# Combined weights of the first two up-projection column tiles, kept in memory apart from the normed x

## The chip, the cores and the metric

The kernel runs on one core of one Trainium2 chip. Its time is the device time of one execution in microseconds (us). A core has five engines that work side by side, each through its own list of instructions: the tensor engine (PE, matmuls and transposes, results in PSUM), the vector engine (DVE), the scalar engine (ACT), GpSimd (POOL) and the sync engine (SP), which here only issues DMA transfers. They wait for one another by semaphores.

## What is computed

Two layers of a transformer trunk on x of 1024 positions by 1024 channels. In each layer a modulated norm and a mixer (attention in layer 0, retention and a state-space model in layer 1) are followed by another modulated norm and a convolutional feed-forward part. The change touches the first half of the last one, the "up" product, and the modulation vector:

```python
def modulated_rmsnorm(x, g, shift, scale):
    y = rmsnorm(x, g) * (1.0 + scale.astype(jnp.float32)[:, None, :]) + shift.astype(jnp.float32)[:, None, :]
    return y.astype(x.dtype)

def conv_ffn(h, w_in, conv_w, conv_b, w_out):
    up = h @ w_in
    val, gate = jnp.split(up, 2, axis=-1)
    gate = lax.conv_general_dilated(gate, conv_w[:, None, :], (1,), [(CONV_W - 1, 0)],
                                    dimension_numbers=('NWC', 'WIO', 'NWC'),
                                    feature_group_count=D_FF) + conv_b
    return (jax.nn.gelu(gate) * val) @ w_out

# in reference(), for each layer i
    mod = cond @ mod_w[i] + mod_b[i]
    sh1, sc1, g1, sh2, sc2, g2 = jnp.split(mod, 6, axis=-1)
```

D_FF is 2816, so `up` has 22 column tiles of 128 for `val` and 22 for `gate`.

## The kernel before

**Precision.** Every matmul operand is split into a high part (`fp32r`, by an ACT copy, L124) and a low part (the rest, a DVE subtraction, L125), and a product is three passes: high by high, high by low, low by high (`mm3`, L134 to L136). A product of four tiles of 128 channels is 12 matmuls of 128x512.

**Order.** The program is written in one sequence; a scheduler puts each engine's instructions into a fixed order when the kernel is built, by the priorities (`high_priority` lifts an operation by `AHEAD` places) and by which buffers are free. Tiles come from pools; a tile with a tag waits until an earlier tile of the same tag (`bufs` of them) has been read for the last time. The chip then runs each engine's list in that order.

**The up phase** (`up7`, L1494) runs once in each layer, here called the first (from about 642 us) and the second (from about 1809 us). It forms the product of two 2x2 block matrices with seven products instead of eight. For column tile `ft` the weights are `g` (of gate) and `a` (of val), each 1024 columns in memory, the first 512 of them for the channels 0 to 511 ("lo"). The blocks of x are B11, B12, B21, B22 and the combinations T1 to T4 of them, kept as high and low parts: B11 and B21 in `h[0]`, T1 and T3 in `h[1]` (both called `h` in rows), B22 in `X0`, T4 and T2 in `X2` (both called `X` in rows). Per column tile:

- `head`: loads g and splits it as A; `p1` = A lo by B11, copied to `s1` by ACT (L1534); `p2` = A hi by B21 (`c1`).
- `sums` (L1540): loads a; four DVE operations of 512 columns (L1545 to L1549) make s3 = g lo − a lo, a combined V and a combined G; V and G are split by L124 and L125.
- `p5` = V lo by T1, `p3` = G hi by B22, `p6` = G lo by T2, `p7` = S3 by T3 (S3 is the split of s3, made in `third`, L1587), `p4` = V hi by T4. `gate0` (L1572) adds p1 and p2 and starts the convolution; `last` finishes the second half.

For the first four tiles (`PRE`) `head`, `p1` and `p2` run first, among the making of the blocks (`up7_blocks`, L1457, a generator whose pieces `next(prep)` lets in). The making normalizes half of xT in place (`scale`), subtracts blocks from each other (L1482, L1486, L1487, L1489, 2048 columns each) and splits each result (`low`, L1479 on ACT and L1480 on DVE): T1, B22, T2, T3, T4. Then `free()` gives xT's memory back, and the pool `late` takes it: V (L1547), `s3h` and `s3l`, the convolution's `ca` and others lie there. PSUM has two banks `c1`, three `c2`, three `c3`; `p1` and `p2` take `c1`, `p6`, `p7`, `p4` and the block making take `c2`, `p5` and `p3` take `c3`. The tag `ma` (2 buffers) holds in turn the sum of squares, s3 and gate0's sum.

**The modulation sums.** `mod_slow` (L535) makes columns of the modulation vector in small steps: one load of 256 KB of `mod_w` into `ms` and one DVE operation into `md` per step (L551, L553), and four matmuls at the end of a column (`mod_cols`). A step is let in by `mod_on`: one per column tile in the up phases (`slow()`), others in the down product, in the mixer and in the output projection. `ms` and `md` have two buffers each in the pool `dp`, which nothing else uses.

Of the kernel before, what the change touches and what calls it, by code (L numbers as in the profile page):

```python
# [25 lines left out]
PRE = 4  # L26
# [69 lines left out]
class Trunk:  # L96
# [438 lines left out]
    def mod_slow(self, todo):  # L535

        nc = self.nc

        def load(l, j, half, t):
            st = self.dp.tile([128, 512], F32, tag="ms", name="ms", bufs=2)  # L540
            c0 = j * 1024 + half * 512
            nc.sync.dma_start(st, self.i["mod_w"][l, t * 128:t * 128 + 128, c0:c0 + 512])
            return st
        steps = [(*c, t) for c in todo for t in range(KD)]
        left, st = [], load(*steps[0])
        where = yield
        for n, (l, j, half, t) in enumerate(steps):
            x, st = st, load(*steps[n + 1]) if n + 1 < len(steps) else None
            if t == 0:
                acc = self.dp.tile([128, 512], F32, tag="md", name="md", bufs=2)  # L550
                nc.vector.tensor_scalar(acc, x, self.cond[:, 0:1], None, ALU.mult)  # L551
            else:
                nc.vector.scalar_tensor_tensor(acc, x, self.cond[:, t:t + 1], acc, ALU.mult, ALU.add)  # L553
            if t == KD - 1:
                left.append((l, j, half, acc))
            elif t == 2 and left:
                c = left.pop()
                self.mod_cols(*c, *where[:2], **where[2])
            where = yield
        yield  # L560
        c = left.pop()
        self.mod_cols(*c, *where[:2], **where[2])
# [894 lines left out]
    def up7_blocks(self, l, xT, ps, tag, xb):  # L1457
# [20 lines left out]
        def low(x, dst):  # L1478
            nc.scalar.activation(dst[:, 0], x, AF.Copy)  # L1479
            v.tensor_tensor(dst[:, 1], x, f(dst[:, 0]), ALU.subtract)  # L1480
# [2 lines left out]
        scale(4)  # L1483
        low(B11, T1)
        low(B22, X0)
        v.tensor_tensor(B12, B22, B12, ALU.subtract)  # L1486
        v.tensor_tensor(B22, B22, B11, ALU.subtract)  # L1487
        low(B22, T2)
# [5 lines left out]
    def up7(self, l, blocks, free, wxs, Gd):  # L1494
# [10 lines left out]
        with self.pool(f"u7ps{l}", bufs=1, space=PSUM) as ps:  # L1505
# [28 lines left out]
                nc.scalar.copy(q["s1"], p)  # L1534

            def p2(ft, q):
                q["c1"] = bank(1)
                product(q["c1"], q["A"], 512, "B21")

            def sums(ft, q):  # L1540
                with self.tc.high_priority(offset=AHEAD):
                    g, a = q["g"], load(wxs, ft * 128)
                    q["s3"] = s3 = self.tmp(tag="ma")
                    lo, hi = slice(0, 512), slice(512, 1024)
                    v.tensor_tensor(s3, g[:, lo], a[:, lo], ALU.subtract)  # L1545
                    v.tensor_tensor(a[:, lo], a[:, lo], a[:, hi], ALU.add)
                    q["V"] = self.split(a, 1024, late)  # L1547
                    v.tensor_tensor(g[:, lo], a[:, lo], g[:, lo], ALU.subtract)
                    v.tensor_tensor(g[:, hi], g[:, hi], g[:, lo], ALU.subtract)  # L1549
                    q["G"] = self.split(g, 1024, self.wp)  # L1550
# [32 lines left out]
            def p3(ft, q):  # L1583
                q["c3"] = bank(3)
                product(q["c3"], q["G"], 512, "B22")
# [35 lines left out]
            for ft in range(PRE):  # L1621
# [7 lines left out]
                if ft > 1:  # L1629
                    c = self.tmp()  # L1630
                    nc.scalar.copy(c, Q[ft]["c1"])
                    Q[ft]["c1"] = c
            operands()
            free()
            with self.pool(f"late{l}", bufs=1) as late:
                for ft in range(2):
                    sums(ft, Q[ft])
                    p5(ft, Q[ft])
                    p3(ft, Q[ft])
                    gate0(ft, Q[ft])  # L1640
                third(0, Q[0])
                for ft in range(NF):
# [4 lines left out]
                        if ft + 2 >= PRE:  # L1647
                            p1(ft + 2, m)
                    p7(ft, q)
                    slow()  # L1650
                    if ft + 1 < NF:
                        third(ft + 1, n)
                    if ft + 2 < NF:
# [199 lines left out]
```

## Time and profile before

| | us |
|---|---|
| median of 3 runs | 2528.89 |
| lowest and highest run | 2512.32 and 2530.38 |
| the profiled execution's own time | 2519.67 |
| its span from first to last instruction | 2518.0 |

The profile is of one execution. It gives the busy time of each engine, tables by stretches of time, the instructions in order of time, and for an engine that sat idle what ended the wait. A row of the order of time begins with the start and the duration in us; a pipelined matmul's duration is longer than its step to the next one. The tensor engine is busy for 96% of the span, DVE for 73%, ACT for 45%. The mean granted clock of the tensor engine is 0.977 of full speed.

### The profile page before, as it was taken

The page shows a single profiled execution, that of the slowest core. Times are in us where ns is not written, and L with a number is a line of the kernel's source. Part 1 is how long each engine was busy: PE and PEld are TensorE (multiplying, and loading weights), DVE is VectorE, ACT ScalarE, POOL GpSimd, SP SyncE. Part 2 cuts the span into 40 slices and gives each one's busy share as a digit, 9 for nine tenths or more (in the row PEclk, how much of TensorE's full clock was granted, in tenths as well). Part 3 has the DMA queues.
Part 4 walks back from the last instruction along what each step waited for, and adds up shares of the span by engine and source line. Part 5 has one row for each costly group of instructions (what it writes and reads, how often), then busy time and mean ns, then how long its engine had stood idle before and what let it go on. Part 6 is the DMA issues. An engine that isn't in the chain of part 4 may idle for free.

```text
span 2518.0 us, 32681 instructions
## 1 busy us (share of the span) xinstructions
PE 2412.1 (96%) x11599; PEld 1985.8 (79%) x11599; DVE 1836.4 (73%) x3383; ACT 1144.7 (45%) x1764; POOL 190.9 (8%) x356
## 2 busy tenths in 40 slices
PE   6999999999899999999989999999989999999997
PEld 5788888887688888888767778887768888878886
DVE  6787766665898788868897554675897888775554
ACT  4556566774544344334443443432454434334442
POOL 1000000032000000000000120201000000000000
PEclk7999999999999999999999999899999999999999
DMA  8565544476132232378676442449522222238562
GB/s 315 153 183 143 146 132 138 143 234 220 59 101 88 88 109 83 102 272 262 219 234 204 153 157 90 159 150 314 170 80 88 76 79 89 84 126 281 178 226 92
DMA packets 323524, 391.56 MB, mean 156 GB/s; under 512 B 28641, under 2 KB 203350, under 8 KB 322848
## 3 DMA queue, kind: packets, MB, share of 16 engines
q1 hardware_dynamic: 294848, 293.45, 37.8%
q0 software_dynamic: 28512, 96.02, 10.6%
q8 instruction: 91, 1.49, 0.3%
q14 instruction: 73, 0.60, 0.1%
HBM read 292.73 MB, written 70.30 MB: 144 GB/s over the span
## 4 chain that ended last, share of the span: by engine, by line
PE 72%; DVE 10%; DMA 8%; issue 4%; ACT 4%; SPq 1%; POOL 1%; DVEq 0%; ACTq 0%; POOLq 0%
PE c L134 11%; PE c L136 11%; PE c L135 10%; PE lin L135 5%; PE lin L134 5%; PE acc L135 5%; PE lin L136 5%; PE acc L136 5%; PE acc L134 5%; DMA ms<-in_mod_w_dram 2%; DVE wL L125 2%; PE ta L775 1%; DMA mix<-mixd 1%; PE S L752 1%; PE S L753 1%
## 5 line engine op out<-in xcount | busy, mean ns | idle before, releaser
L124 ACT ACTIVATE wH<-stage 128x1024 fp32r<-128x1024 f32 x372 | 392.7, 1059 | 522.4 <-PE acc L136 149.3
L125 DVE TENSOR_TENSOR wL<-stage,wH 128x1024 fp32r<-128x1024 f32 x372 | 452.9, 1220 | 195.1 <-ACT wH L124 190.6
L135 PE MATMUL acc<-wL,wH 128*128 128x512 f32 x704 | 278.8, 396 | 9.9 <-DVE wL L125 9.9
L136 PE MATMUL acc<-wH,wL 128*128 128x512 f32 x704 | 278.5, 396 | 0.0
L134 PE MATMUL acc<-wH 128*128 128x512 f32 x704 | 272.8, 394 | 5.4 <-ACT wH L124 5.1
L134 PE MATMUL lin<-h,wH 128*128 128x512 f32 x576 | 233.3, 405 | 7.6 <-ACT h L422 6.6
L135 PE MATMUL lin<-h,wH 128*128 128x512 f32 x576 | 233.0, 405 | 0.0
L136 PE MATMUL lin<-h,wL 128*128 128x512 f32 x576 | 230.1, 400 | 0.0
L134 PE MATMUL c<-h,wH 128*128 128x512 f32 x528 | 210.8, 399 | 15.9 <-ACT wH L124 6.8
L135 PE MATMUL c<-X,wH 128*128 128x512 f32 x528 | 206.5, 391 | 2.8 <-DVE X L1480 2.8
L136 PE MATMUL c<-h,wL 128*128 128x512 f32 x528 | 208.6, 395 | 0.6 <-DVE wL L125 0.5
L135 PE MATMUL c<-h,wH 128*128 128x512 f32 x528 | 208.1, 394 | 0.0
L134 PE MATMUL c<-X,wH 128*128 128x512 f32 x528 | 206.2, 391 | 0.2 <-ACT t2k L1581 0.2
L136 PE MATMUL c<-X,wL 128*128 128x512 f32 x528 | 205.4, 391 | 0.0
L135 PEld LDWEIGHTS acc<-wL,wH 128*128 128x128 f32 x704 | 133.9, 190 | 42.0 <-DVE wL L125 14.4
L134 PEld LDWEIGHTS acc<-wH 128*128 128x128 f32 x704 | 133.5, 190 | 34.1 <-ACT wH L124 6.0
L136 PEld LDWEIGHTS acc<-wH,wL 128*128 128x128 f32 x704 | 133.9, 190 | 27.6
L134 PEld LDWEIGHTS c<-h,wH 128*128 128x128 f32 x528 | 100.4, 190 | 44.4 <-ACT wH L124 10.4
L134 PEld LDWEIGHTS lin<-h,wH 128*128 128x128 f32 x576 | 109.9, 191 | 28.6 <-ACT h L422 6.9
L135 PEld LDWEIGHTS lin<-h,wH 128*128 128x128 f32 x576 | 110.0, 191 | 20.2 <-DVE h L425 1.4
L136 PEld LDWEIGHTS lin<-h,wL 128*128 128x128 f32 x576 | 109.9, 191 | 20.1 <-issue 0.4
L136 PEld LDWEIGHTS c<-h,wL 128*128 128x128 f32 x528 | 100.3, 190 | 26.2 <-DVE wL L125 2.3
(508 smaller groups left out, 5010.7 us busy)
## 6 DMA issues: line engine op xcount, KB each, us to landing
stage<-in_ffn_w_in_dram SPq DMA_DIRECT2D x92, 512.0 KB, 3.9
stage<-in_ffn_w_out_dram SPq DMA_DIRECT2D x176, 256.0 KB, 3.9
stage<-Gd SPq DMA_DIRECT2D x176, 256.0 KB, 4.0
ms<-in_mod_w_dram SPq DMA_DIRECT2D x104, 256.0 KB, 3.5
Gd<-ca POOLq DMA_DIRECT2D x88, 256.0 KB, 2.8
pn<-in_mod_w_dram SPq DMA_DIRECT2D x56, 256.0 KB, 3.6
mix<-mixd POOLq DMA_DIRECT2D x52, 256.0 KB, 5.8
stage<-in_ev_w_in_dram SPq DMA_DIRECT2D x24, 512.0 KB, 3.9
```

Source lines behind the costliest of these rows:

```text
L124: nc.scalar.activation(wh[:, :n], st[:, :n], AF.Copy)
L125: nc.vector.tensor_tensor(wl[:, :n], st[:, :n], f(wh[:, :n]), ALU.subtract)
L134: nc.tensor.matmul(ps, wh, xh, start=s, stop=False)
L135: nc.tensor.matmul(ps, wh, xl, start=False, stop=False)
L136: nc.tensor.matmul(ps, wl, xh, start=False, stop=e)
L752: nc.tensor.matmul(dst, q, KH[:, kk], start=True, stop=False)
L753: nc.tensor.matmul(dst, q, KL[:, kk], start=False, stop=True)
L775: nc.tensor.transpose(pt[:, kk, j * 128:j * 128 + 128], W[j][:, (a + kk) * 128:(a + kk) * 128 + 128], self.ident)
```

## The change

The making of the blocks gets one more stop, after B22. After the products p1 and p2 of the first four tiles, `sums`, `p5` and `p3` of the first two tiles now come before `free()` and the late pool, the rest of the making between them. Since the late pool is not there yet, V of tile 0 goes to the tag `w` of the pool `wxs` (one buffer, in which A of tiles 0 and 2 lies as well) and V of tile 1 to new tiles `wH`, `wL` of the pool `dp`. `mod_slow` uses these same tiles of `dp`, half of each at a time, in place of `ms` and `md`, and takes them only at its first step; the up phases let in a step only from the third tile on. p2 of tiles 2 and 3 takes bank `c2` instead of `c1`. `gate0` stays behind the late pool.

```diff
--- before.py
+++ after.py
@@ -536,8 +536,11 @@
 
         nc = self.nc
 
+        where = yield
+        stage, acc = (f(self.dp.tile([128, 1024], F32R, tag=t, name=t, bufs=1)) for t in ("wH", "wL"))
+
         def load(l, j, half, t):
-            st = self.dp.tile([128, 512], F32, tag="ms", name="ms", bufs=2)
+            st = stage[:, t % 2 * 512:t % 2 * 512 + 512]
             c0 = j * 1024 + half * 512
             nc.sync.dma_start(st, self.i["mod_w"][l, t * 128:t * 128 + 128, c0:c0 + 512])
             return st
@@ -547,12 +550,12 @@
         for n, (l, j, half, t) in enumerate(steps):
             x, st = st, load(*steps[n + 1]) if n + 1 < len(steps) else None
             if t == 0:
-                acc = self.dp.tile([128, 512], F32, tag="md", name="md", bufs=2)
-                nc.vector.tensor_scalar(acc, x, self.cond[:, 0:1], None, ALU.mult)
+                a = acc[:, n // KD % 2 * 512:n // KD % 2 * 512 + 512]
+                nc.vector.tensor_scalar(a, x, self.cond[:, 0:1], None, ALU.mult)
             else:
-                nc.vector.scalar_tensor_tensor(acc, x, self.cond[:, t:t + 1], acc, ALU.mult, ALU.add)
+                nc.vector.scalar_tensor_tensor(a, x, self.cond[:, t:t + 1], a, ALU.mult, ALU.add)
             if t == KD - 1:
-                left.append((l, j, half, acc))
+                left.append((l, j, half, a))
             elif t == 2 and left:
                 c = left.pop()
                 self.mod_cols(*c, *where[:2], **where[2])
@@ -1483,6 +1486,7 @@
         scale(4)
         low(B11, T1)
         low(B22, X0)
+        yield
         v.tensor_tensor(B12, B22, B12, ALU.subtract)
         v.tensor_tensor(B22, B22, B11, ALU.subtract)
         low(B22, T2)
@@ -1534,7 +1538,7 @@
                 nc.scalar.copy(q["s1"], p)
 
             def p2(ft, q):
-                q["c1"] = bank(1)
+                q["c1"] = bank(2 if 1 < ft < PRE else 1)
                 product(q["c1"], q["A"], 512, "B21")
 
             def sums(ft, q):
@@ -1544,7 +1548,7 @@
                     lo, hi = slice(0, 512), slice(512, 1024)
                     v.tensor_tensor(s3, g[:, lo], a[:, lo], ALU.subtract)
                     v.tensor_tensor(a[:, lo], a[:, lo], a[:, hi], ALU.add)
-                    q["V"] = self.split(a, 1024, late)
+                    q["V"] = self.split(a, 1024, *((wxs, "w", 1) if ft == 0 else (self.dp, "w", 1) if ft == 1 else (late,)))
                     v.tensor_tensor(g[:, lo], a[:, lo], g[:, lo], ALU.subtract)
                     v.tensor_tensor(g[:, hi], g[:, hi], g[:, lo], ALU.subtract)
                     q["G"] = self.split(g, 1024, self.wp)
@@ -1631,12 +1635,15 @@
                     nc.scalar.copy(c, Q[ft]["c1"])
                     Q[ft]["c1"] = c
             operands()
+            for ft in range(2):
+                sums(ft, Q[ft])
+                p5(ft, Q[ft])
+                p3(ft, Q[ft])
+                if ft == 0:
+                    next(prep)
             free()
             with self.pool(f"late{l}", bufs=1) as late:
                 for ft in range(2):
-                    sums(ft, Q[ft])
-                    p5(ft, Q[ft])
-                    p3(ft, Q[ft])
                     gate0(ft, Q[ft])
                 third(0, Q[0])
                 for ft in range(NF):
@@ -1647,7 +1654,8 @@
                         if ft + 2 >= PRE:
                             p1(ft + 2, m)
                     p7(ft, q)
-                    slow()
+                    if ft > 1:
+                        slow()
                     if ft + 1 < NF:
                         third(ft + 1, n)
                     if ft + 2 < NF:
```

The tensor engine in the first up phase, before: the last three matmuls of p2 of tile 3 (`c_7124`), and behind them the first three of p6 of tile 0 (`c_7251`, from `X`, block T2).

```order
L134 MATMUL c_7124<-h,wH 128x512
L135 MATMUL c_7124<-h,wH 128x512
L136 MATMUL c_7124<-h,wL 128x512
L134 MATMUL c_7251<-X_6556,wH 128x512
L135 MATMUL c_7251<-X_6556,wH 128x512
L136 MATMUL c_7251<-X_6556,wL 128x512
```

In the order of before all eight products p1 and p2 of the first four tiles stand ahead of these rows.

The tensor engine at the same place of the changed kernel: the end of p6 of tile 0 (`c_7249`), three matmuls of p7 of tile 0 (`c_7266`), and the start of p1 of tile 2 (`c_7062`).

```order
L134 MATMUL c_7249<-X_6554,wH 128x512
L135 MATMUL c_7249<-X_6554,wH 128x512
L136 MATMUL c_7249<-X_6554,wL 128x512
L134 MATMUL c_7266<-h,s3h 128x512
L135 MATMUL c_7266<-h,s3h 128x512
L136 MATMUL c_7266<-h,s3l 128x512
L134 MATMUL c_7062<-h,wH 128x512
L135 MATMUL c_7062<-h,wH 128x512
L136 MATMUL c_7062<-h,wL 128x512
```

p1 of tiles 2 and 3 has moved behind p6 of tile 0, so six products stand ahead of it; behind p1 of tile 3 come p5 and p3 of tile 0, p5 and p3 of tile 1, the rest of p7 of tile 0, and p4 of tile 0. The second up phase has the same order.

DVE in the first up phase, before, from gate0's addition of tile 0 on (L1574; L1475 is the normalizing, L1548 and L1549 are operations of `sums`, L1482, L1486, L1487 and L1489 the block subtractions, L1480 the low parts of T1, B22, T3, T2 and T4).

```order
L1574 TENSOR_TENSOR ma<-c_6984,pn 128x512
L125 TENSOR_TENSOR wL<-stage,wH 128x1024
L1475 SCALAR_TENSOR_TENSOR xT<-xT,gs_91,c_6997 128x512 x6
L1482 TENSOR_TENSOR xT<-xT 128x4x512
L1475 SCALAR_TENSOR_TENSOR xT<-xT,gs_91,c_6997 128x512 x2
L1548 TENSOR_TENSOR stage<-stage 128x512
L1549 TENSOR_TENSOR stage<-stage 128x512
L1480 TENSOR_TENSOR h<-xT,h 128x2048
L1486 TENSOR_TENSOR xT<-xT 128x4x512
L1480 TENSOR_TENSOR X_6555<-xT,X_6555 128x2048
L1480 TENSOR_TENSOR h<-xT,h 128x2048
L1487 TENSOR_TENSOR xT<-xT 128x4x512
```

Behind these rows stand a split (L125), the subtraction L1489 and the low parts of T2 and T4.

DVE of the changed kernel from the second half of the normalizing on (L1549 to L1553 are the operations of `sums`, L1483 the low parts, L1490, L1491 and L1493 block subtractions).

```order
L1553 TENSOR_TENSOR stage<-stage 128x512
L1549 TENSOR_TENSOR ma<-stage 128x512
L1483 TENSOR_TENSOR h<-xT,h 128x2048
L125 TENSOR_TENSOR wL<-stage,wH 128x1024
L1550 TENSOR_TENSOR stage<-stage 128x512
L1483 TENSOR_TENSOR X_6553<-xT,X_6553 128x2048
L125 TENSOR_TENSOR wL<-stage,wH 128x1024
L1552 TENSOR_TENSOR stage<-stage 128x512
L1490 TENSOR_TENSOR xT<-xT 128x4x512
L1553 TENSOR_TENSOR stage<-stage 128x512
L1491 TENSOR_TENSOR xT<-xT 128x4x512
L1483 TENSOR_TENSOR h<-xT,h 128x2048
```

The four operations of the sums of tile 1 and the splits of G of tile 0 and V of tile 1 now stand among the low parts; gate0's additions (L1578) stand behind all of them, after `s3l`, and the subtraction that T4 needs (L1493; L1489 before) stands behind the low part of T2.

ACT of the changed kernel, from the high part of B22 on (L1635 copies p2 of tile 3, L1482 are the high parts of T3, T2 and T4, L1594 is `s3h`, L1538 copies p1 of tile 2).

```order
L1482 ACTIVATE X_6553<-xT 128x2048
L1635 COPY t2k<-c_7113 128x512
L124 ACTIVATE wH<-stage 128x1024
L1482 ACTIVATE h<-xT 128x2048
L1482 ACTIVATE X_6554<-xT 128x2048 x2
L1594 ACTIVATE s3h<-ma 128x512
L1559 ACTIVATE ca<-ma,colsB,taps 128x512
L1564 COPY halo<-ma 128x2
L1569 ACT_TABLE_LOAD
L1569 ACTIVATE ca<-ca 128x512
L124 ACTIVATE wH<-stage 128x1024
L1538 COPY pn<-c_7062 128x512
```

Before, the copies of p1 and p2 of tiles 2 and 3 stood among the high parts; now those of p1 stand behind `s3h` and the first gelu.

Of the 104 operations of the modulation sums, 16 stood on DVE ahead of the first output projection's end and stand now among the column tiles 4 to 8 of the first up phase; 16 that stood around the last output projection stand among the tiles 4 to 8 of the second up phase.

## Rows read from the trace of the kernel before

**Rows 1.** The page: busy us of each engine, its share, and instructions.

```profile
PE 2412.1 (96%) x11599; PEld 1985.8 (79%) x11599; DVE 1836.4 (73%) x3383; ACT 1144.7 (45%) x1764; POOL 190.9 (8%) x356
```

**Rows 2.** Stretches: length, busy us per engine (PE, PEld, DVE, ACT, POOL), clock, DMA.

```profile
642.00:706.00 64.00, 55.72 (x224) 42.39 (x223) 57.66 (x73) 35.74 (x45) 1.08 (x2) 0.92 0.25 73
706.00:1080.00 374.00, 374.00 (x1651) 306.80 (x1652) 309.00 (x475) 150.01 (x213) 21.58 (x40) 1.00 0.29 92
1815.00:1865.00 50.00, 39.56 (x156) 30.14 (x155) 46.28 (x47) 29.49 (x35) 0.00 (x0) 0.90 0.18 53
1865.00:2230.00 365.00, 365.00 (x1614) 299.73 (x1614) 294.99 (x451) 148.76 (x212) 20.52 (x38) 1.00 0.26 83
```

**Rows 3.** PE in order of time: start, duration; in brackets the wait ahead.

```profile
665.47 0.80 PE L134 MATMUL c<-h,wH 128*128 128x512 f32 x1 [3.23 <-ACT t2k L1631]
...
677.70 0.50 PE L135 MATMUL c<-X,wH 128*128 128x512 f32 x1 [2.80 <-DVE X L1480]
...
696.64 0.39 PE L134 MATMUL c<-X,wH 128*128 128x512 f32 x1
...
1827.60 0.50 PE L134 MATMUL c<-h,wH 128*128 128x512 f32 x1 [3.15 <-ACT pn L1534]
...
1845.50 0.80 PE L134 MATMUL c<-h,wH 128*128 128x512 f32 x1 [5.90 <-ACT wH L124]
...
1864.14 0.39 PE L134 MATMUL c<-X,wH 128*128 128x512 f32 x1
```

**Rows 4.** PE by single us: length, busy us, matmuls, granted clock.

```profile
666.00:667.00 1.00, 1.00 (x4) 0.50 0.00 0
672.00:673.00 1.00, 1.00 (x6) 1.00 0.00 0
```

**Rows 5.** DVE in order of time, the making of the blocks in both up phases.

```profile
650.24 0.68 DVE L1574 TENSOR_TENSOR ma<-c,pn 128x512 f32<-128x512 f32 x1
650.84 1.22 DVE L125 TENSOR_TENSOR wL<-stage,wH 128x1024 fp32r<-128x1024 f32 x1
651.97 4.03 DVE L1475 SCALAR_TENSOR_TENSOR xT<-xT,gs,c 128x512 f32<-128x512 f32 x6
...
673.16 2.28 DVE L1489 TENSOR_TENSOR xT<-xT 128x2048 f32<-128x2048 f32 x1
675.37 4.48 DVE L1480 TENSOR_TENSOR X<-xT,X 128x2048 fp32r<-128x2048 f32 x2
...
1839.71 4.64 DVE L1480 TENSOR_TENSOR X<-xT,X 128x2048 fp32r<-128x2048 f32 x2
```

**Rows 6.** ACT in order of time, first up phase: high part of T4, and s3h.

```profile
675.48 1.91 ACT L1479 ACTIVATE X<-xT 128x2048 fp32r<-128x2048 f32 x1 [0.18 <-DVE xT L1489]
...
680.85 0.62 ACT L1590 ACTIVATE s3h<-ma 128x512 fp32r<-128x512 f32 x1
```

**Rows 7.** Stretches, instructions on md alone: PE, PEld, DVE busy us and count.

```profile
60.00:180.00 120.00, 0.00 (x0) 0.00 (x0) 11.20 (x16) 0.96 0.59 171
...
880.00:1080.00 200.00, 1.89 (x16) 2.09 (x16) 11.42 (x16) 1.00 0.30 97
1752.00:1812.00 60.00, 0.00 (x0) 0.00 (x0) 11.44 (x16) 1.00 0.62 206
```

**Rows 8.** Waits of DVE, 1752 to 1812 us: total, times, longest.

```profile
DVE md L553 <- DMA ms<-in_mod_w_dram: 10.5, 4, 5.3
```

**Rows 9.** PE in order of time, in the last output projection.

```profile
1785.79 0.43 PE L611 MATMUL lin<-ident,rs 128*128 128x128 f32 x2 [2.83 <-DVE rs L224]
```

**Rows 10.** ACT in order of time: one step (L845) of each of four attention units.

```profile
131.67 0.62 ACT L845 ACTIVATE t2k<-t2k 128x512 fp32r<-128x512 f32 x1
...
192.19 0.62 ACT L845 ACTIVATE t2k<-t2k 128x512 fp32r<-128x512 f32 x1
...
251.56 0.63 ACT L845 ACTIVATE t2k<-t2k 128x512 fp32r<-128x512 f32 x1 [0.25 <-DVE t2k L837]
...
310.43 0.63 ACT L845 ACTIVATE t2k<-t2k 128x512 fp32r<-128x512 f32 x1
```

## The prediction

> **What bounds the kernel now.** I read the busy totals first, then the table by stretches, then the waits of the stretches that are not full. The tensor engine (PE) is busy for 2412.1 of 2518.0 us [rows 1], so the place to look is where it is not. Both up phases are full from their third column tile on: 374.00 us of 374 and 365.00 of 365 [rows 2]. That also gives a duration: 374.00 us for 1651 matmuls is 0.2265 us each, 2.72 us for a product of 12. The idle time sits at the head of each up phase, while the blocks of x are made: 64.00 − 55.72 = 8.3 us in the first and 50.00 − 39.56 = 10.4 us in the second [rows 2]. The reader is to see what ends it: PE waits for a PSUM copy (3.23 us) and then 2.80 us for `X`, the low part of block T2; in the second phase 3.15 us for a copy and 5.90 us for `wH`, the split of the first combined weights [rows 3]. After a wait of that size the granted clock stands at 0.50, 1.2 GHz instead of 2.4, for about one product [rows 4].
>
> The work that sets the end of the head is the vector engine's (DVE): from 650.24 to T2's low part at 675.37 + 2.2 = 677.6 it has one instruction behind the other [rows 5]. (The row of two lasts 4.48, so one is 2.2; from start to start an addition of 512 columns takes 0.60 and a split of 1024 columns 1.13.)
>
> **The heads, part by part.** PE takes its matmuls as they stand, so the orders in the section on the change decide. Before, eight products stand ahead of p6(0), the one that needs T2. Afterwards there are six: p1(2) and p1(3) have moved behind it. The reason is a chain of buffers. `gate0(0)` and `gate0(1)` take a `ma` buffer, and with both `sums` ahead of them the two buffers hold s3(0) and s3(1) until `third(0)` splits s3(0); its `s3h`, `s3l` lie in the late pool, which lies where xT was, so it waits for the last block, T4. Until gate0 is done both buffers of bank 1 are held, and p1(2), p1(3) have none. V(0) in `wxs` replaces the A weights of tile 2, which p1(2) reads, so p5(0) comes behind p1(2) as well, and p3(0), p5(1), p3(1) stand behind p5(0). So the products that the change could have made early stand last.
>
> T2 itself. Up to it DVE gains four operations of 512 columns (the second tile's sums) and one 1024 column split, and loses gate0's addition and, to a place behind T2, the subtraction L1489: 3 × 0.65 + 1.13 − 2.2 = +0.9 us [rows 5] (0.65 lies between the step of 0.60 and the duration of 0.68). T2 comes at 678.5. From there the chain is new: L1493 2.2, ScalarE's (ACT's) copy of T4 1.9 [rows 6], its low part 2.2, so T4 at 684.8; ACT's `s3h` 0.6 [rows 6], DVE's `s3l` 0.6 and gate0(0) 0.6, with the waits between them: p1(2) starts at 687.1. PE has then done p6(0) and three matmuls of p7(0). Six products (16.3) and nine matmuls (2.0) follow until p4(0); p5(0) waits another 0.7 for V(0), whose ACT part stands behind the table load and the gelu of gate0. p4(0) starts at 706.1 where it started at 696.64 [rows 3]: **+9.5**. All products that were ahead of it before are ahead of it now, so this is the loss, and as PE was full behind it, nothing gives it back. If the clock is still at half when p1(2) starts, a product costs up to 5.1 instead of 2.7, but in part hidden by gate0(1): +1.5. I take **+10.3** between the two.
>
> In the second phase the old chain held one split and four small operations ahead of T2, so the addition is 4 × 0.65 + 2 × 1.13 − 2.2 = +2.7: T2 at 1839.71 + 2.2 + 2.7 = 1844.6 [rows 5], p1(2) 8.6 later at 1853.2, p4(0) 19.0 after that at 1872.2 against 1864.14 [rows 3]: +8.1, with the clock +9.6; I take **+8.8**.
>
> On the clock, the rows show 0.50 after a wait of 3.23 us and 1.00 again within the next product [rows 4], and the new waits are longer. The Trainium skill (TensorE: Matmul & The Clock Gate, section "HAM oscillation — how this bites in real kernels") says that a gap long enough drops the clock again each time, so that the slow stretch is paid per gap. By that rule alone each head would have the full 1.5 and the sum would be 1.5 us higher; by the rows, half.
>
> **The modulation sums.** 104 DVE operations keep their number; the loads move with them. Now 16 of them (11.20 us) run in the attention between 60 and 180 us, and 16 (11.44 us) between 1752 and 1812 [rows 7]. Afterwards the first 16 run in tiles 4 to 8 of the first up phase and 16 in tiles 4 to 8 of the second, since they take the memory of V(1). In the output projection ahead of the second up phase they stood between the steps of the inverse root, where PE waits 2.83 us [rows 9]; without them and their waits for loads (10.5 us over four [rows 8]) that wait goes: **−2.8** (bounds 0 and −2.8). In the attention the order becomes that of the last of the first four units for all of them: the spacing of the units falls from 60.52 over 59.37 to 58.87 us [rows 10]; at 58.87 for all, 1.65 + 0.50 go: **−2** (bounds −2.2, and +2 if the new order puts a stall in). The new places: two column tiles are 2 × 84 × 0.2265 = 38.1 us of PE, in which DVE, without the sums that it already has there, is busy (309.00 − 11.42)/374 = 80%, 30.3 us [rows 2, 7]; 8 sums more at 0.71 are 5.7. That is 36.0 of 38.1, hidden behind PE, but barely: **0** (bounds 0 and the rival below).
>
> Bank 2 for two copies, two calls of the slow sums less, one send more: no instruction added, the copies stay on ACT, which is busy 150 of 374 us [rows 2]. 0.
>
> **Sum.** 10.3 + 8.8 − 2.8 − 2.0 = +14.3 us, **0.6%**. On the profiled execution, 2519.67 us, that is 2534.0. It lies 9.2 us under the median of the three runs, 2528.89, which themselves spread over 18 us; on the median the sum is 2543. I give 2538, halfway.
>
> **Rivals.**
> - *DVE overfull in tiles 4 to 8.* If 5 of the 16 sums there wait for their loads as the four did, 2.6 us each [rows 8], 13 us stand against the 2 × 2.1 us that are free: +9 in each up phase, 2556. It decides when the waits pass 2.1 us per two tiles. For it: the waits in the rows. Against it: the 16 sums that already run between 880 and 1080 us left PE full [rows 2, 7].
> - *The gaps are filled* (faster). If p5(0), p3(0), p5(1) and p3(1) ran while the blocks are made, the idle 8.3 + 10.4 would go with the 4.8 above, and with it the slow clock, by estimate two products in each head at 2.7 us more: 2519.67 − 34 = 2485. For it: V and G of tile 0 and V of tile 1 no longer wait for xT. Against it: the order, and V(0)'s place. It decides at whether PE waits at p6(0) for less than 2.80 us instead of some 9 us more.
> - *Nothing comes of it.* The two heads lose only what the added DVE work costs, 0.9 and 2.7, since p1(2), p1(3) fit in other gaps, and the gains of 4.8 cancel it: 2519 to 2529. Against it: the rows of p7(0) and p1(2) behind p6(0).
>
> **How the numbers follow.** 1% is about what a measurement of this kernel can tell from no change. Chances: the forecast, slower but within 1%: 0.72; DVE overfull, beyond 1%: 0.17 with the upper ends of the heads; no difference: 0.07; filled: 0.04. So faster 0.04, within 1% 0.79, slower 0.17. The range runs from the third rival's low end to the first rival's: 2518 to 2560; leaving out the filled case and half of the first keeps 8 in 10.
>
> **What would show it.** In the profile after: PE idle at the first p6(0) for some 16 to 18 us in one piece, ended by `X` of the block making; then p7(0) waiting for `s3h`; p1(2) ending not before 689; p4(0)'s matmul about 9 us later relative to the head's first product. In the second phase the same, with the 2.83 us wait at the transposes of `rs` gone. Wrong, if PE shows a p5 or p3 product ahead of p6(0), if the head's idle time is under 15 us, or if stretches 720 to 880 us are not full.

## The result, and the profile after

The changed kernel takes 2545.99 us (median of five runs, 2543.45 to 2548.04); the kernel before, run beside it, 2528.79 (2512.32 to 2530.38). The ratio is 1.009, with a 95% interval from 1.0067 to 1.0113: slower, by just under 1%. The predicted time was 2538, in a range from 2518 to 2560. The profiled execution took 2543.45 us.

The page of the changed kernel, its span and PE's busy time, which answer [rows 1]:

```profile
span 2541.7 us, 32684 instructions
...
PE 2414.4 (95%) x11599; PEld 1992.2 (78%) x11599; DVE 1837.2 (72%) x3383; ACT 1145.9 (45%) x1764; POOL 191.3 (8%) x356
```

PE has the same 11599 matmuls; of the 23.7 us that the span grew 2.3 are busy and 21.4 idle time of PE. The table by stretches, the columns as in [rows 2]: the first head, the rest of the first up phase, the same of the second.

```profile
642.00:706.00 64.00, 45.03 (x181) 34.78 (x181) 51.14 (x60) 32.04 (x39) 0.54 (x1) 0.84 0.24 70
706.00:1080.00 374.00, 373.60 (x1643) 305.38 (x1642) 312.05 (x479) 151.46 (x216) 21.68 (x40) 1.00 0.31 97
1823.00:1887.00 64.00, 45.15 (x181) 35.27 (x182) 50.30 (x59) 31.25 (x38) 0.54 (x1) 0.84 0.24 70
1890.00:2255.00 365.00, 364.83 (x1608) 299.09 (x1607) 302.61 (x464) 149.15 (x213) 21.15 (x39) 1.00 0.29 92
```

The heads are idle for 64.00 − 45.03 = 19.0 and 64.00 − 45.15 = 18.9 us, where it was 8.3 and 10.4 [rows 2]. Behind them both phases are as full as before. PE in order of time, the matmuls that answer [rows 3]: the first product, the waits, the first p1(2), the first p4(0), for each phase.

```profile
641.83 0.39 PE L134 MATMUL c<-h,wH 128*128 128x512 f32 x1
...
675.25 0.79 PE L134 MATMUL c<-X,wH 128*128 128x512 f32 x1 [14.81 <-ACT X L1482]
...
677.71 0.80 PE L135 MATMUL c<-X,wH 128*128 128x512 f32 x1 [1.67 <-DVE X L1483]
...
684.84 0.50 PE L134 MATMUL c<-h,s3h 128*128 128x512 f32 x1 [2.39 <-ACT s3h L1594]
...
686.30 0.79 PE L134 MATMUL c<-h,wH 128*128 128x512 f32 x1
...
705.92 0.39 PE L134 MATMUL c<-X,wH 128*128 128x512 f32 x1
...
1823.07 0.47 PE L134 MATMUL c<-h,wH 128*128 128x512 f32 x1 [0.94 <-ACT wH L124]
...
1856.07 0.79 PE L134 MATMUL c<-X,wH 128*128 128x512 f32 x1 [14.80 <-ACT X L1482]
...
1867.12 0.79 PE L134 MATMUL c<-h,wH 128*128 128x512 f32 x1
...
1886.86 0.39 PE L134 MATMUL c<-X,wH 128*128 128x512 f32 x1
```

The first product of each phase in the kernel before:

```profile
642.75 0.39 PE L134 MATMUL c<-h,wH 128*128 128x512 f32 x1
...
1809.17 0.47 PE L134 MATMUL c<-h,wH 128*128 128x512 f32 x1 [0.94 <-ACT wH L124]
```

In the changed kernel PE reaches p6(0) after six products and waits 14.81 + 1.67 us for T2, then 2.39 for `s3h`, and only then has p1(2). DVE in order of time shows what lets p1(2) go: T2's low part, T4's, then `s3l`, then gate0's addition (L1578), which frees a buffer of bank 1 at 685.55 + 0.69 = 686.24.

```profile
675.37 2.28 DVE L1483 TENSOR_TENSOR X<-xT,X 128x2048 fp32r<-128x2048 f32 x1
...
681.83 2.29 DVE L1483 TENSOR_TENSOR X<-xT,X 128x2048 fp32r<-128x2048 f32 x1 [1.98 <-ACT X L1482]
...
684.84 0.68 DVE L1595 TENSOR_TENSOR s3l<-ma,s3h 128x512 fp32r<-128x512 f32 x1
685.55 0.69 DVE L1578 TENSOR_TENSOR ma<-c,pn 128x512 f32<-128x512 f32 x1
```

From the first product to p4(0) it is 705.92 − 641.83 = 64.1 us in the first phase, 53.9 before (642.75 to 696.64): +10.2. In the second 63.8 against 55.0 (1809.17 to 1864.14): +8.8. In all four cases 180 matmuls stand between the two, so these differences compare the same work. That leaves 4.7 of the 23.7, and the place is found by the same subtraction at the next landmark, the first residual of the down projection (a DVE row, 1145.66 before, 1159.33 after): 453.4 us from p4(0) to there instead of 449.0, **+4.4**. From there to the first product of the second phase it is +0.2, behind the second p4(0) +1.0, in the stretch up to the first product of all −0.9.

The +4.4 lie where the first up phase ends. All rows from here are of the changed kernel unless the sentence ahead says otherwise. PE in order of time has one long wait there:

```profile
1104.80 0.79 PE L135 MATMUL acc<-wL,wH 128*128 128x512 f32 x1 [5.23 <-DVE wL L125]
```

The sync engine's queue in order of time just ahead of it, merged by line:

```profile
1094.30 7.50 SPq L545 DMA_DIRECT2D wH<-in_mod_w_dram  x5
1101.90 0.38 SPq L1690 DMA_DIRECT2D stage<-in_ffn_w_out_dram  x1
```

DVE in order of time, two of the sums (L556) that wait, and the splits (L125) behind them:

```profile
1099.35 0.75 DVE L556 SCALAR_TENSOR_TENSOR wL<-wH,small,wL 128x512 f32<-128x512 f32 x1 [1.00 <-DMA wH<-in_mod_w_dram]
...
1102.86 0.75 DVE L556 SCALAR_TENSOR_TENSOR wL<-wH,small,wL 128x512 f32<-128x512 f32 x1 [1.41 <-DMA wH<-in_mod_w_dram]
1103.52 2.35 DVE L125 TENSOR_TENSOR wL<-stage,wH 128x1024 fp32r<-128x1024 f32 x2
```

The table by stretches there:

```profile
1092.00:1114.00 22.00, 16.31 (x68) 13.09 (x67) 15.50 (x23) 7.70 (x8) 1.08 (x2) 0.84 0.78 253
```

The stretch that answers it in the kernel before:

```profile
1082.00:1104.00 22.00, 20.92 (x94) 17.08 (x93) 14.79 (x22) 9.60 (x10) 1.08 (x2) 0.92 0.73 250
```

And, also before, the sync engine's load that answers the one at 1101.90:

```profile
1089.13 0.52 SPq L1682 DMA_DIRECT2D stage<-in_ffn_w_out_dram  x1
```

A column of slow modulation sums now falls on the start of the down projection. On SP five loads of `mod_w` stand in one piece ahead of the fifth weight load, which issues at 1101.90 instead of 1089.13 (3.5 us later, counted from p4(0)). On DVE the sums, each behind its load, stand ahead of the weight splits (L125), and PE waits 5.23 us for one of these. Which of the two queues does it, the experiments had to say.

### The profile page after: what moved, and what is told of

It is laid out like the page before. It is cut to its first block, busy times and chain, and to the rows that moved or that the text cites. A ratio compares the mean times of both kernels' runs of the same rounds, so it can differ in the third digit from the quotient of the medians.

```text
span 2541.7 us, 32684 instructions
## 1 busy us (share of the span) xinstructions
PE 2414.4 (95%) x11599; PEld 1992.2 (78%) x11599; DVE 1837.2 (72%) x3383; ACT 1145.9 (45%) x1764; POOL 191.3 (8%) x356
## 4 chain that ended last, share of the span: by engine, by line
PE 69%; DVE 11%; issue 8%; DMA 7%; ACT 3%; SPq 1%; POOL 1%; DVEq 0%; ACTq 0%; POOLq 0%
PE c L136 10%; PE c L134 10%; PE c L135 10%; PE lin L134 5%; PE lin L135 5%; PE lin L136 5%; PE acc L135 5%; PE acc L136 5%; PE acc L134 5%; DMA wH<-in_mod_w_dram 2%; DVE wL L125 2%; PE ta L778 1%; PE S L755 1%; PE S L756 1%; DVE wL L556 1%
## 5 line engine op out<-in xcount | busy, mean ns | idle before, releaser
L125 DVE TENSOR_TENSOR wL<-stage,wH 128x1024 fp32r<-128x1024 f32 x372 | 453.3, 1220 | 192.0 <-ACT wH L124 183.9
L134 PEld LDWEIGHTS c<-X,wH 128*128 128x128 f32 x528 | 100.2, 190 | 51.7 <-ACT X L1482 30.5
```

What stands on the lines that cost most here:

```text
L125: nc.vector.tensor_tensor(wl[:, :n], st[:, :n], f(wh[:, :n]), ALU.subtract)
L134: nc.tensor.matmul(ps, wh, xh, start=s, stop=False)
```

## The experiments

Each line of the table is one profiled execution, cut at landmarks that every kernel has, in us: the start of the first up phase's first product; from there to the addition of p4(0) on DVE (the head); to the first residual of the down projection; to the first product of the second up phase; to the addition of p4(0) there (the second head); to the end. Before, p4's matmuls are mixed with p5's, and its addition comes 5.6 us behind its first matmul; in the changed kernel 3.2. So a head's loss by this column is 2.4 us smaller than by the matmul in the first phase, and the next column larger by as much. The expectations count the changed kernel and most of its variants to the wait just ahead of that addition, 0.5 us earlier: 66.8, 66.5, 450.7 and 443.9 there are 67.3, 67.0, 450.2 and 443.4 here.

| kernel | start | head | to residual | to phase 2 | head 2 | to end | span | ratio to before (95%) |
|---|---|---|---|---|---|---|---|---|
| before | 642.8 | 59.5 | 443.4 | 663.5 | 58.2 | 650.6 | 2518.0 | |
| before again (e11) | 644.0 | 58.8 | 442.5 | 669.7 | 59.3 | 651.4 | 2525.7 | |
| changed | 641.8 | 67.3 | 450.2 | 663.7 | 67.0 | 651.6 | 2541.7 | 1.009 (1.0067 to 1.0113) |
| changed again (e10) | 642.5 | 67.6 | 449.9 | 661.1 | 66.9 | 651.8 | 2539.7 | |
| e1 sums late | 645.0 | 59.5 | 447.0 | 661.0 | 59.2 | 648.6 | 2520.4 | 0.9998 (0.9984 to 1.0013) |
| e2 one tile early | 644.5 | 55.7 | 447.3 | 664.3 | 55.8 | 649.5 | 2517.2 | 0.9975 (0.9963 to 0.9987) |
| e3 additions apart | 642.3 | 55.5 | 446.0 | 663.9 | 54.7 | 647.1 | 2509.5 | 0.9953 (0.9934 to 0.9973) |
| e4 fewer slow steps | 642.6 | 66.9 | 443.4 | 667.2 | 66.8 | 652.0 | 2538.9 | 1.0071 (1.0052 to 1.009) |
| e5 loads by GpSimd | 643.2 | 67.4 | 460.3 | 691.1 | 67.1 | 651.8 | 2580.9 | 1.0199 (1.0167 to 1.0232) |
| e6 = e3 and e4 | 645.9 | 55.1 | 441.1 | 664.8 | 54.8 | 648.6 | 2510.3 | 0.995 (0.9935 to 0.9966) |
| e7 blocks in one piece | 642.3 | 67.3 | 449.7 | 664.7 | 66.7 | 651.8 | 2542.5 | 1.0076 (1.0046 to 1.0107) |
| e8 = e3 and e5 | 646.9 | 56.7 | 455.0 | 682.3 | 55.3 | 649.2 | 2545.3 | 1.0071 (1.0046 to 1.0095) |
| e9 = e3, copies from bank 1 | 643.4 | 56.2 | 446.3 | 665.9 | 55.4 | 647.8 | 2515.0 | 0.9958 (0.994 to 0.9976) |

**e10 and e11, both kernels again.** What one execution can tell comes first, since every other line is read against it.

> The changed kernel once more, unaltered, for the spread of the terms between two executions. Theory: the heads (66.8 and 66.5 us to the addition of p4(0)) and the way from there to the first residual of the down projection (450.7) repeat within 0.7 us; the start of the first up phase (641.83) moves by up to 4, as it does between the kernels that have the same order up to there (641.8 to 645.9), so that an attention term of 1 or 2 us can't be read from one execution.

> The kernel before once more, unaltered. Theory: heads of 59.5 and 58.2 us to the addition of p4(0) and 443.4 from there to the first residual repeat within 0.7 us; the first up phase starts somewhere between 641 and 646 (642.75 in the profile before). Rival (the moved sums do make the attention regular and shorter): it starts at 643 or later here, and the changed kernel's again at or under 642.

The heads repeat within 1.2 us and the way to the residual within 1; for the kernel before that is more than the 0.7 expected. The start does not, and the long stretch to phase 2 neither. PE's first product of the first phase, in order of time, in the changed kernel's repeat:

```profile
642.54 0.39 PE L134 MATMUL c<-h,wH 128*128 128x512 f32 x1
```

The same in the repeat of the kernel before:

```profile
644.01 0.39 PE L134 MATMUL c<-h,wH 128*128 128x512 f32 x1
```

The same in e6, whose instructions stand in the changed kernel's order up to there:

```profile
645.91 0.39 PE L134 MATMUL c<-h,wH 128*128 128x512 f32 x1
```

With that order the start lies anywhere from 641.8 to 645.9, and the kernel before is at 642.8 and 644.0 among them. The rival, a start that the change makes earlier, finds nothing in these rows.

**e1, the early sums undone, the moved modulation sums kept.**

```diff
...
+            next(prep)
             free()
             with self.pool(f"late{l}", bufs=1) as late:
                 for ft in range(2):
+                    sums(ft, Q[ft])
+                    p5(ft, Q[ft])
+                    p3(ft, Q[ft])
                     gate0(ft, Q[ft])
```

> The changed kernel with the sums of the first two tiles, p5 and p3 put back behind the freeing of xT, in the old order with gate0; V(1) stays in the pool of the slow modulation sums, so those keep their new places. Theory (the buffers): the two heads lose only because both ma buffers hold s3(0) and s3(1), which holds bank 1; so here the heads take what they took before, 53.9 us from the first product to p4(0) in the first phase and 55.0 in the second (64.1 and 63.8 in the changed kernel), and what is left is the cost of the moved modulation sums: 23.7 - 10.2 - 8.8 = +4.7 us, a span of 2522 to 2524, with the wait of some 5 us at the start of the first down projection still there. Rival 1 (the term of my prediction): the moved sums gain 4.8, span 2513. Rival 2 (the heads lose by another part of the change, the V tile or the block making in two parts): the heads stay at 60 or more, span 2535 to 2542.

The heads are those of before. The wait at the down projection is there (447.0 against 443.4 and 442.5), and the kernel as a whole is level with before. So the heads' loss comes from the early sums and what this run takes back with them, V(0)'s place in `wxs` and the stop in the block making, for which e2, e3 and e7 stand; the moved modulation sums bring nothing and cost nothing that the times can tell, neither the 4.8 that I gave them nor the whole 4.7 expected here (the interval goes from −4.0 to +3.3 us). What the down projection loses is within what the stretch behind it varies.

**e2, only tile 0 early.** V(0) keeps its place in `wxs`, and one `ma` buffer stays free for gate0.

```diff
...
-            for ft in range(2):
-                sums(ft, Q[ft])
...
+            sums(0, Q[0])
+            p5(0, Q[0])
+            p3(0, Q[0])
+            next(prep)
             free()
...
+                gate0(0, Q[0])
+                sums(1, Q[1])
...
```

> The changed kernel with only tile 0's sums, p5 and p3 ahead of the freeing of xT; tile 1's come after it. Then s3(0) takes one ma buffer and gate0(0) the other, bank 1 comes free early, and the order has p1(2), p1(3), p5(0) and p3(0) ahead of p6(0). Theory (the buffers): the heads fall from 64.1 and 63.8 to 49 to 54 us from first product to p4(0), under the 53.9 and 55.0 of the kernel before, since two products more stand ahead of p6(0); span 2541.7 - 2 x (10 to 14) = 2514 to 2522. Rival (the vector engine: the combined weights made among the blocks delay T2, or V(0) waits for the weights of tile 2): the heads stay at 58 to 64, span 2532 to 2542.

**e3, gate0's additions apart.** Both tiles' sums stay early, gate0 no longer asks for `ma`, and V(1) and p5(1) come behind `free()`.

```diff
...
                 p2(ft, Q[ft])
+                if ft == 0:
+                    cc = f(self.dp.tile([128, 1024], F32R, tag="wL", name="wL", bufs=1))
+                if ft < 2:
+                    Q[ft]["c"] = cc[:, ft * 512:ft * 512 + 512]
+                    v.tensor_tensor(Q[ft]["c"], Q[ft]["c1"], Q[ft]["s1"], ALU.add)
...
             with self.pool(f"late{l}", bufs=1) as late:
+                Q[1]["V"] = self.split(Q[1]["a"], 1024, late)
                 for ft in range(2):
                     gate0(ft, Q[ft])
+                p5(1, Q[1])
```

> The changed kernel with the additions of gate0(0) and gate0(1) done right behind p2 into the tile that V(1) had, and V(1) made after xT is free; both tiles' sums, p5(0), p3(0) and p3(1) stay early. No ma buffer is asked for by gate0. Theory (the buffers): p1(2) and p1(3) stand ahead of p6(0) again, and p5(0), p3(0) too; heads of 48 to 54 us, span 2512 to 2522, like the kernel with one tile early. If the second tile's sums on the vector engine ahead of T2 cost what the prediction gave them (three additions and a split, about 3 us), each head is up to 3 us longer than with one tile. Rival (the vector engine's work ahead of T2 makes the loss): 58 to 64 us, span 2532 to 2542.

Both bring the heads from 67 to 54 to 56 us, under those of before, by two different cures of the same thing: a buffer of bank 1 that comes free early. Gate0's first addition, at 685.55 in the changed kernel, in e2 (DVE in order of time):

```profile
651.99 0.68 DVE L1578 TENSOR_TENSOR ma<-c,pn 128x512 f32<-128x512 f32 x1
```

And in e3:

```profile
649.57 0.68 DVE L1638 TENSOR_TENSOR wL<-c,pn 128x512 f32<-128x512 f32 x1
```

V(0) has the changed kernel's place in both, and e3 has the second tile's sums among the blocks as well, so neither of these makes the loss. Both also take V(1)'s split and p5(1) from among the blocks, and no run puts those back alone; the split is 1.13 us of DVE. The idle time of e3's first head is two waits for T2 and no more (PE in order of time):

```profile
675.37 0.50 PE L134 MATMUL c<-X,wH 128*128 128x512 f32 x1 [3.88 <-ACT X L1482]
...
679.04 0.80 PE L135 MATMUL c<-X,wH 128*128 128x512 f32 x1 [3.16 <-DVE X L1483]
```

T2 comes 679.04 − 642.26 = 36.8 us after the first product, in e2 33.8 (678.39 − 644.55): the second tile's four operations of `sums` and gate0's second addition, which e3 has ahead of T2 and e2 has not, cost 2.9 us, about what the expectation named for three additions and a split. They are earned back by p3(1), which PE does behind p6(0) while it waits for T4, and e3's heads are shorter than e2's by 0.2 and 1.1. e3's span, 2509.5, lies under the expected range.

**e4, fewer slow steps in the first up phase.**

```diff
-                    if ft > 1:
+                    if ft > 1 and (l or ft < 14):
                         slow()
...
-                    hooks = {s: [...] for s in range(2, 26)}
+                    hooks = {s: [...] for s in range(2, 36)}
...
```

> The changed kernel with the slow modulation sums not called in the last eight column tiles of the first up phase; the steps left over run in the first down projection. In the sync engine's queue one load of mod_w instead of six then stands ahead of the fifth weight load of the down projection. Theory (the queue): the 4.4 us lost between p4(0) of the first up phase and the first residual of the down projection (453.4 us against 449.0 before) come from those loads, which wait for the vector engine's sums and hold the weight loads behind them; here 449 to 450.5 us, span 2537 to 2539. Rival (the vector engine is overfull at the end of the up phase or the sums cost the same wherever they stand): 453 us or the loss comes back in the down projection, span 2541 to 2543.

The sync engine's queue at that place in e4:

```profile
1097.65 0.35 SPq L545 DMA_DIRECT2D wH<-in_mod_w_dram  x1
1098.09 0.38 SPq L1690 DMA_DIRECT2D stage<-in_ffn_w_out_dram  x1
```

The loss is gone (443.4). Of the 6.8 us, 3.5 are back in the next column, which is within that column's own spread, and the time is the changed kernel's within the intervals.

**e5, the loads of the sums issued by GpSimd; e8, the same on e3.** If weight loads held up in SP's queue were the cause, this should help.

```diff
-            nc.sync.dma_start(st, self.i["mod_w"][l, ...])
+            nc.gpsimd.dma_start(st, self.i["mod_w"][l, ...])
```

> The changed kernel with the loads of the slow modulation sums issued from GpSimd's queue instead of the sync engine's; nothing else. Theory (the sync queue): the loss at the start of the first down projection comes from weight loads that stand behind mod_w loads in the sync engine's queue, so it goes: from p4(0)'s addition in the first up phase to the first residual of the down projection 443 to 445 us instead of 450.7 (443.4 before; 443.9 with fewer steps in the up phase), and unlike there nothing comes back later: span 2534 to 2537. Rival 1 (the vector engine's queue): the sums wait for their loads ahead of the weight splits just as before, 449 to 451, span 2540 to 2542. Rival 2: GpSimd's queue also carries the stores of the up phase's output; a mod_w load that waits there holds them up, and the down projection starts later still, span 2543 to 2550.

> The kernel with gate0's additions apart and V(1) late, with the loads of the slow sums in GpSimd's queue. Theory (the sync queue): 2509.5 minus what the loads in GpSimd's queue alone bring (5 to 7), 2503 to 2505. Rival 1 (vector engine's queue): 2508 to 2510. Rival 2 (the stores of the up phase are held up): 2511 to 2518.

Both lose, 1.1 points against the changed kernel and 1.2 against e3, and lie beyond every expectation. In e5 the weight load is issued early; SP in order of time:

```profile
1097.62 0.35 SPq L1690 DMA_DIRECT2D stage<-in_ffn_w_out_dram  x1
```

And still PE waits for splits; e5's waits of PE from 1085 to 1400 us (total, times, longest):

```profile
PE acc L135 <- DVE wL L125: 21.4, 9, 7.6
```

DVE's waits of the same stretch in e5, for the loads of the sums:

```profile
DVE wL L556 <- DMA wH<-in_mod_w_dram: 28.3, 16, 4.1
```

The same view of the changed kernel:

```profile
DVE wL L556 <- DMA wH<-in_mod_w_dram: 9.7, 8, 2.7
```

With SP's queue clear, the scheduler put 16 sums instead of 8 into the first 46 us of the down projection, and each waits for its own load ahead of a weight split. So my theory of the sync queue fell: it is DVE's queue. The changed kernel's own rows say so once one looks: the split that PE waits for at 1104.80 starts at 1103.52, right behind the last waiting sum. ACT had made its high part by 1097.28 + 1.04 = 1098.32, 5.2 us earlier (the changed kernel, ACT in order of time):

```profile
1097.28 1.04 ACT L124 ACTIVATE wH<-stage 128x1024 fp32r<-128x1024 f32 x1
```

And behind 1104.80 PE has no wait over 0.25 us until the residual at 1159.33, so the late weight loads in SP's queue cost it nothing there. The stage has two halves, so a load is issued only when the sum two before has read its half; a run of sums goes at the pace of the transfers and holds what stands behind it. GpSimd's stores, the second rival, are not what PE waits for in these rows.

The first 46 us are the smaller part of e5's loss: against the changed kernel the column to the residual grows by 10.1 us, the next one, to phase 2, by 27.4. The longest wait of PE in that part is in the output projection, for a residual (L1446) that stands on DVE behind sums waiting for their loads (e5, PE in order of time):

```profile
1791.66 0.77 PE L134 MATMUL lin<-mix,wH 128*128 128x512 f32 x1 [10.38 <-DVE xT L1446]
```

How much of the 27.4 comes from DVE's order and how much from GpSimd's queue, in which the loads now stand among other transfers, is not separated.

**e6, e3 and e4 together.**

> The kernel with gate0's additions apart and V(1) late, together with the slow sums not called in the last eight tiles of the first up phase. Theory: the two causes are independent, so the gains add: against the changed kernel 32.2 (additions apart) and 2.9 (fewer steps) in the profiled span, 2541.7 - 35 = 2506 to 2508; heads 54 to 55 us to the addition of p4(0), 443 to 445 from there to the first residual. Rival (they share slack): the gain at the first down projection comes back in full, span 2509 to 2511.

The parts add up in their own columns (heads 55.1 and 54.8, 441.1 to the residual), but the sum cannot be told from e3: the span lies in the rival's range, its start comes 3.6 us later with the same order up to there, and the intervals overlap. e2, e3, e6 and e9 beat both kernels, e3 and e6 by the most, 0.5% under before.

**e7, the blocks in one piece.** The `yield` in the block making and its `next(prep)` are taken out of the changed kernel.

> The changed kernel with the blocks made in one piece again (the stop between T1's and T2's parts taken out). On the vector engine the second tile's sums then stand behind T2 and T4 instead of among them. My prediction gave the stop 2.2 us of T2's time; T2 should come 0.9 earlier here (3.1 of sums move behind it, one subtraction of 2.2 moves ahead of it) and T4 3.1 earlier. Theory (the chain of buffers): what PE waits for is gate0, which stands behind the sums as well as behind T4, so p1(2) starts where it did within 1.5 us and the heads stay at 65.5 to 67.5 us to the addition of p4(0) (66.8 and 66.5 in the changed kernel), span 2539 to 2543. Rival (the making of the blocks alone sets the head): T4 3.1 earlier gives 3 us in each head, span 2535 to 2537.

PE in order of time in its first head:

```profile
677.45 0.80 PE L135 MATMUL c<-X,wH 128*128 128x512 f32 x1 [2.80 <-DVE X L1483]
...
686.23 0.80 PE L136 MATMUL c<-h,s3l 128*128 128x512 f32 x1 [3.17 <-DVE s3l L1594]
```

T2 is 0.8 us earlier counted from the first product (677.45 − 642.33 against 677.71 − 641.83), and the heads are the same: what T4 gains stands as sums ahead of `s3l`, for which PE now waits. The stop alone moves nothing.

**e9, p2's copies from bank 1 again, on e3.**

> The kernel with gate0's additions apart and V(1) late, with p2 of the third and fourth tile written to bank 1 again instead of bank 2. Theory (my prediction for that edit: 0): bank 1 comes free early here, so the product of the fourth tile waits at most for one copy; the heads stay at 54 to 56 us to the addition of p4(0), span 2508 to 2513. Rival (two buffers are too few): p1(3) or p2(3) waits for the copy of c(2) on ScalarE, 1 to 3 us in each head, span 2512 to 2516.

The heads are 0.6 and 0.7 longer, and one new wait of that size (0.68) stands in each, less than the rival's 1 to 3; in the time it doesn't show. I had given that edit 0.

## Why the prediction was right, and where it was not

- **The order as the cause: right, shown.** Six products ahead of p6(0), p1(2) behind T4 and gate0, because s3(0) and s3(1) hold both `ma` buffers. e2 and e3 each set a `ma` buffer or bank 1 free early, and the loss goes.
- **The first head, +10.3: measured +10.2.** The changed kernel's first product comes 0.92 us earlier (641.83 against 642.75). With that added back, T2, put at 678.5, came at 678.57 (675.37 + 2.28 + 0.92), T4, put at 684.8, at 685.04, p1(2), put at 687.1, at 687.22 and p4(0), put at 706.1 without the clock, at 706.84. The wait for V(0), 0.7, did not show, and the clock cost 0.55 more than was taken for it; that these two nearly cancel is luck.
- **The second head, +8.8: measured +8.8.**
- **The clock: half taken, nearly the whole came.** From p1(2) to p4(0) are 81 matmuls, 18.35 us at 0.2265; they took 19.62 and 19.74, so 1.3 and 1.4 where I had 0.75. The granted clock in short stretches, the third column from the end: at half behind the long wait, at full by 682.0, and at half once more behind the wait of 2.39. So the slow start of p1(2) is not left over from the long wait, as the prediction had it, but follows the shorter one.

```profile
677.70:679.70 2.00, 1.99 (x5) 1.62 (x6) 2.00 (x1) 0.00 (x0) 0.00 (x0) 0.50 0.00 0
...
682.00:682.50 0.50, 0.45 (x2) 0.01 (x1) 0.50 (x1) 0.00 (x0) 0.00 (x0) 1.00 0.00 0
...
685.50:686.00 0.50, 0.50 (x2) 0.29 (x1) 0.47 (x2) 0.00 (x0) 0.00 (x0) 0.50 0.00 0
...
689.30:692.00 2.70, 2.70 (x14) 2.22 (x13) 0.51 (x2) 2.69 (x5) 0.00 (x0) 1.00 0.00 0
```

  The Trainium skill (TensorE: Matmul & The Clock Gate, section "HAM oscillation — how this bites in real kernels") says that a gap long enough drops the clock again each time it comes. The row of 0.50 behind the wait of 14.81 us agrees, and the rows show such a fall behind the wait of 2.39 us as well.
- **The output projection, −2.8: the wait went, the gain did not.** The row that answers [rows 9], the second one here, has no wait. A new one of 1.84 us stands at the start of the same projection, for an operation (L1422) that has sums on DVE ahead of it, and the granted clock is 0.67 in the three us after it. PE in order of time:

```profile
1725.48 0.47 PE L134 MATMUL lin<-mix,X 128*128 128x512 f32 x1 [1.84 <-DVE pn L1422]
...
1799.74 0.60 PE L614 MATMUL lin<-ident,rs 128*128 128x128 f32 x4
```

  I had taken away the sums of the second phase and not asked where the sums of the mixer would then stand. What is left of the term lies below the spread of 6.2 us that this stretch has between two executions of one kernel.
- **The attention, −2: wrong mechanism.** The order did become regular (the second and third of the spacings hold the same instructions in the same order on PE, DVE and ACT), but the spacing is 59.96, 59.58 and 59.95 us in the rows that answer [rows 10], and the last one's 58.87 was no floor that the others reach; the three together take 179.5 us where they took 178.8:

```profile
132.26 0.62 ACT L848 ACTIVATE t2k<-t2k 128x512 fp32r<-128x512 f32 x1
...
192.22 0.63 ACT L848 ACTIVATE t2k<-t2k 128x512 fp32r<-128x512 f32 x1
...
251.80 0.63 ACT L848 ACTIVATE t2k<-t2k 128x512 fp32r<-128x512 f32 x1
...
311.75 0.63 ACT L848 ACTIVATE t2k<-t2k 128x512 fp32r<-128x512 f32 x1
```

- **The moved sums in tiles 4 to 8, 0: right there, and blind to the next place.** The stretch that answers [rows 7], the sums of L556 alone (DVE busy and count; two more are the first of a column, L554):

```profile
720.00:800.00 80.00, 10.49 (x14) 1.00 0.45 145
```

  PE stays full there. The cost came 300 us later, where the fourth column of sums, shifted with the first two, met the start of the down projection: +4.4, in no term and no rival of mine. The rival "DVE overfull" had the mechanism, sums that wait for their loads, and the wrong place.
- **The sum.** +14.3 was predicted on the profiled execution, where +23.7 came, and on the medians +17.2. The missing 9.4 in the profile are the 4.4, the 4.8 of gains less the 0.9 that showed, and small ends. The range held because the two heads, 19.0 of the 23.7, were right; the two gains did not come. The profiled execution of before was a short one, as e11 shows (2525.7 where it was 2518.0).

What stays open: why the start of the first up phase differs by 4 us between executions with the same order, and the stretch to phase 2 by 6.

## What to carry to other kernels

When work is moved earlier, list every buffer tag that it holds and for how long; a tag of two that is also asked for by a small step further on can move whole products to the back of a fixed order, and the cure (here gate0's addition into another tile, with V(1) made later) is small beside the change. A run of small steps that wait for transfers was harmless here in the middle of the up phase, where PE stayed full, and cost time at the start of the down projection and, in e5, in the output projection, so a shift of it has to be followed to the end of the program and not only to its new place. Repeat one profile before reading single-microsecond terms out of a subtraction.

## What the runs showed of the hardware

A load issued through another engine's queue did not help: GpSimd's loads of 256 KB land in 3.7 us (median), SP's in 3.5, and what cost time at the start of the down projection was the order in which DVE waits for them. The Trainium skill (DMA: Bandwidth & Descriptors, section "Anatomy of one DMA — SWDGE (gpsimd) path") says that a semaphore wait of a transfer is spent on the issuing engine before it goes out; the row of five loads that fill 7.50 us of SP's queue, with issues of 0.33 to 0.35 us each, agrees.

Two executions of the kernel before differ by 7.7 us in span, and 6.2 of it lie in one stretch, while the heads repeat within 1.2.
